# Decay tables of the retention moved from the filter stage to the convolutions; the first normalised input split between VectorE and ScalarE

## The chip, the core and the metric

One core of a Trainium2 chip runs the whole step. The metric is the time of one execution in microseconds on the device, median of several runs. Names of engines: PE is TensorE (matmuls), DVE is VectorE, ACT is ScalarE, POOL is GpSimd, SP issues most DMAs.

## What is computed

Two layers of a hybrid mixer, for a prompt of 128 tokens and a sample of 512, both of width 1024. Cut to what matters here:

```python
def mixer_layer(x, mod, ..., filt, norm_g, w_in, ret_logit, ...):
    h = rmsnorm(x, norm_g) * (1 + scale) + shift
    z = h @ w_in                                  # 5120 columns
    ret_out, ret_s = retention_mixer(q, k, v, ret_logit, ret_s0)
    hy_out = hyena_mixer(zh, hy_conv_w, hy_conv_b, filt, hy_bias)
    lru_out, lru_s = rglru_mixer(...)
    y = concat(ret_out * silu(g_r), hy_out * silu(g_h), lru_out * silu(g_l))
    return x + gate * (y @ w_out), ret_s, lru_s

def retention_dir(q, k, v, log_gamma, state0):    # forward and backward, 4 heads
    dmat = where(diff >= 0, exp(log_gamma * max(diff, 0)), 0)   # 128 x 128 a head
    zeta = exp(log_gamma * (C - 1 - idx))
    xi = exp(log_gamma * (idx + 1.0))
    chunk_decay = exp(log_gamma * C)
    ...
# hyena_filters: a small network over L positions gives two filters a channel;
# the long convolutions with them are done by transforms, twice in a row
```

`dmat`, `xi`, `zeta` and `chunk_decay` are the decay tables. They hang on the weight `ret_logit` alone, so they can be made at any time before the retention.

## The kernel before

All activations lie channels first, with prompt and sample side by side: a tile of 128 channels has 644 columns (128 + 512 and pads). The input projection runs in 40 tiles of output channels (`mtile`; tile names `z0_16` and so on, layer and number, `z_16` for short). Products are kept near full precision by splitting each operand into a high part and a low part: `w_16h`, `w_16l`, and for the normalised input `hh` and `hl`, eight tiles each. A projection tile is 48 matmuls of 322 columns.

Layer 0 goes through these stages. First come a sine network (`hidden`), the norm of the input (`norm0`) and the modulation (`ada_gen`); `make_h0` then makes `hh` and `hl`: for each of eight tiles an affine step from `x` into `t` in two pieces (128 and 512 columns), the high part on ACT, the low part as a difference. Then the filter stage (`filters`): four units `u` one after the other, each with taps (tile `hg`, line 630), a normalisation of them (lines 634 to 645), transposes (`ft`), a fold (lines 508 to 515), splits (`blocks`, line 540) and transforms (`spr`, `spi`). Projection tiles run in between on PE. Then the convolutions (`hy_conv`), in two halves of the channels with two convolutions each, 00 and 01 and then 02 and 03: a fold, splits, five classes that are transformed (`u020` and so on), multiplied by the filter's spectrum (lines 971 to 979), and transformed back (`ie`, `ip`, `io`), and a tail (lines 1047 to 1070) that gives the input of the next fold. Then retention (`ret`) and the recurrent branch (`lru`), head by head, and the output projection.

What sets the order: the work is written as Python generators. `pump` and `until` step those that are due by a planner's clock `clk`, which each matmul advances by its own computed length; a generator says at each `yield` how long it should sleep by that clock. `queue` ties every matmul behind the one before, so PE runs exactly in the order in which the generators issue. `join(t)` steps the generators until `t` is done, and sets the clock forward where nothing is due. The other engines' orders are made by a scheduler from priorities (the order of issue) and dependencies; each engine then takes its instructions strictly in that order.

The tables before: `decays` (some 55 instructions of 8 to 32 columns on DVE) turns the logits into the scales of the exponentials; the scheduler puts it at the program's start. `ret_tables` is a generator started with a delay of 40 (`LTB`) as the layer begins; `ret_table` makes one layer's tables in two steps (directions), each with eight ACTIVATEs of 258 columns on ACT, three tensor_scalar or products on POOL and two steps of 1032 columns on DVE (lines 1111 and 1112), and writes them to DRAM. `prep`, which comes before the convolutions, waits for it and loads them back (`load_tables`).

## Time and profile before

| | us |
|---|---|
| median of 3 runs (1309.91 to 1315.7) | 1310.69 |
| the profiled execution | 1310.14 |
| its span, first to last instruction | 1308.4 |
| PE busy in it | 1159.8 (89%) |
| DVE busy | 896.8 (69%) |
| POOL busy | 627.4 (48%) |
| ACT busy | 590.3 (45%) |

The profiled execution is 0.6 us under the median; 1.7 us of it lie outside the span. Reading: PE is busy for most of the span, but the stages have different limits, so a share of the span says little; what matters is, stage by stage, how long each engine works and what PE waits for.

### The profile page before, as it was taken

Reading aid. Unit: us, or ns where it says so; the run is one execution under the profiler, and the core shown is the slowest. Engines: PE = TensorE matmul, PEld = TensorE weight load, DVE = VectorE, ACT = ScalarE, POOL = GpSimd, SP = SyncE. Lnnn points to the kernel's source line nnn. Section 1 sums busy time; section 2 is a strip of 40 time slices with the busy share of each in tenths; the row PEclk is TensorE's granted clock in tenths of the full one; section 3 lists DMA queues with packets and bytes.
Section 4 is the critical chain, followed back from the end, with each engine's and each line's share of the span. In section 5 each row is a group of like instructions: output and inputs, shape, how many; then the busy total and the mean of one; then the engine's idle time right before and its main releaser. Section 6 shows DMA issues by size and latency. Waiting matters only on the chain. (4 is left out here: it accounts for less than half of the span.)

```text
span 1308.4 us, 20560 instructions
## 1 busy us (share of the span) xinstructions
PE 1159.8 (89%) x7944; PEld 1102.3 (84%) x7944; DVE 896.8 (69%) x1398; ACT 590.3 (45%) x1067; POOL 627.4 (48%) x523
## 2 busy tenths in 40 slices
PE   4588688998998988898989899999999889889996
PEld 2377678998998988897888788999998889879996
DVE  6998976666686776667888775566567587676313
ACT  3567556333333654465565554332333356555221
POOL 2754645544555543634343355544355474445431
PEclk9799879999999988899999989999999899889998
DMA  9642234232211111243545354222221111113222
GB/s 332 218 158 81 80 104 139 93 104 74 73 57 61 41 45 45 79 141 115 176 143 186 122 211 143 79 66 92 77 75 49 53 57 49 47 57 124 64 70 81
DMA packets 53313, 132.79 MB, mean 101 GB/s; under 512 B 6278, under 2 KB 15126, under 8 KB 51936
## 3 DMA queue, kind: packets, MB, share of 16 engines
q1 hardware_dynamic: 52868, 131.38, 30.3%
q8 instruction: 62, 1.02, 0.3%
q14 instruction: 35, 0.29, 0.1%
q10 hardware_dynamic: 348, 0.11, 0.0%
HBM read 112.77 MB, written 18.70 MB: 100 GB/s over the span
## 5 line engine op out<-in xcount | busy, mean ns | idle before, releaser
L298 ACT ACTIVATE r<-arena 128x512 fp32r<-128x512 f32 (+1 forms) x72 | 43.5, 606 | 106.9 <-DVE arena L515 37.6
L298 ACT ACTIVATE arena<-arena 128x644 f32<-128x644 f32 (+6 forms) x88 | 66.1, 766 | 50.4 <-DVE arena L1381 28.6
L298 ACT ACTIVATE rt<-arena 128x512 fp32r<-128x512 f32 (+2 forms) x44 | 29.7, 675 | 77.2 <-POOL arena L976 50.3
L540 POOL TENSOR_TENSOR r<-arena,r 128x512 fp32r<-128x512 f32 (+1 forms) x24 | 29.9, 1245 | 71.6 <-ACT r L298 55.3
L330 PE MATMUL u<-r,cfwd 128*128 128x256 f32 x432 | 61.0, 290 | 2.1 <-DVE r L540 1.9
L330 PEld LDWEIGHTS u<-r,cfwd 128*128 128x128 f32 x432 | 56.8, 197 | 2.8 <-DVE r L540 2.1
L1381 DVE SCALAR_TENSOR_TENSOR arena<-o,arena 128x128 f32<-128x128 f32 (+3 forms) x34 | 16.7, 524 | 56.0 <-PE o L330 56.0
L330 PE MATMUL spr<-r,cfwd 128*128 128x256 f32 x192 | 37.4, 306 | 18.9 <-DVE rt L630 7.6
L971 DVE TENSOR_TENSOR arena<-u,arena 128x512 f32<-128x512 f32 x40 | 27.5, 687 | 38.0 <-PE u L330 36.8
L330 PEld LDWEIGHTS spr<-r,cfwd 128*128 128x128 f32 x192 | 29.4, 199 | 25.5 <-DVE rt L630 9.1
L976 POOL TENSOR_TENSOR arena<-arena 128x256 f32<-128x256 f32 x40 | 36.8, 920 | 21.8 <-DVE arena L972 12.2
L1300 POOL MEMSET arena<- 128x2 f32 x32 | 2.1, 100 | 86.3 <-ACT arena L298 86.3
L979 POOL TENSOR_TENSOR rt<-arena,rt 128x512 fp32r<-128x512 f32 x24 | 31.4, 1308 | 23.9 <-ACT rt L298 23.9
L298 ACT ACTIVATE r<-rt 128x512 fp32r<-128x512 f32 (+3 forms) x50 | 28.2, 564 | 23.2 <-PE spi L330 11.9
L979 DVE TENSOR_TENSOR rt<-arena,rt 128x512 fp32r<-128x512 f32 x16 | 20.4, 1277 | 24.3 <-ACT rt L298 24.3
L298 ACT ACTIVATE arena<-z 64x512 f32<-64x512 f32 (+1 forms) x42 | 26.5, 630 | 23.5 <-PE z L330 23.1
L330 PE MATMUL hg<-r 128*128 128x320 f32 x128 | 26.3, 343 | 11.8 <-DVE r L587 9.5
L540 POOL TENSOR_TENSOR r<-rt,r 128x256 fp32r<-128x256 f32 (+1 forms) x16 | 20.1, 1256 | 34.5 <-ACT r L298 27.8
L330 PE MATMUL spi<-r,cfwd 128*128 128x256 f32 x168 | 34.8, 297 | 1.2 <-DVE rt L630 1.2
L1152 DVE TENSOR_TENSOR rt<-rt,arena 128x512 f32<-128x512 f32 x16 | 23.8, 1490 | 17.4 <-POOL arena L1151 17.4
L1199 DVE TENSOR_TENSOR arena<-rs,dm 128x512 f32<-128x512 f32 (+1 forms) x16 | 7.1, 486 | 40.7 <-PE rs L330 40.7
L298 ACT ACTIVATE arena<-lg,arena 128x322 f32<-128x322 f32 x64 | 30.3, 529 | 10.4 <-PE lg L330 10.1
(1269 smaller groups left out, 4285.8 us busy)
## 6 DMA issues: line engine op xcount, KB each, us to landing
w<-in_w_in SPq DMA_DIRECT2D x80, 512.0 KB, 3.9
aw<-in_ada_w SPq DMA_DIRECT2D x96, 256.0 KB, 5.2
wo<-in_w_out SPq DMA_DIRECT2D x32, 384.0 KB, 3.3
spec<-arena SPq DMA_DIRECT2D x16, 640.0 KB, 3.3
arena<-spec SPq DMA_DIRECT2D x8, 1280.0 KB, 5.4
arena<-in_xT SPq DMA_DIRECT2D x16, 320.0 KB
rt<-in_c_win SPq DMA_DIRECT2D x4, 640.0 KB, 6.3
arena<-xspill SPq DMA_DIRECT2D x8, 320.0 KB, 3.5
```

What stands on the lines that cost most here:

```text
L298: return S.activation(out, in_, f, bias=bias, scale=scale)
L330: return queue(T.matmul(out, lhs, x, start=start, stop=stop), w * n / 2400 * (4 if x.dtype == F32 else 1))
L540: eng.tensor_tensor(lo, src, f(h), op=ALU.subtract)
L971: V.tensor_tensor(y, pv, hre[:, c].unsqueeze(1).broadcast_to([P, 2, 256]), op=ALU.mult)
L976: G.tensor_tensor(y[:, 1], y[:, 1], m2[:, 0], op=ALU.add)
L979: (G if PY >> c & 1 else V).tensor_tensor(lo, yo, f(h), op=ALU.subtract)
L1152: V.tensor_tensor(q, q, ar(sw, 512), op=ALU.add)
L1199: V.tensor_tensor(ar(SC_R + 128 * s0, 128 * nb).rearrange("p (n c) -> p n c", n=nb), ps[:, 0:128 * nb].rearrange("p (n c) -> p n c", n=nb) ...
L1300: G.memset(ar(tt[d] + c, 2), 1.0)
L1381: V.scalar_tensor_tensor(x, zc(ps, pc, pc + n), ar(mod_[l] + 32 + 2 * mt + s, 1), x, op0=ALU.mult, op1=ALU.add)
```

## The change

Four things. (1) `decays` is now the first thing that `ret_tables` issues, and its scratch has moved from the region `HS_` to `ZB_`, where `norm0` keeps its sum (`ACC_`). (2) `ret_tables` starts when `prep` of layer 0 is through, so beside the convolutions. It works in pieces of two heads instead of four (516 columns, twice as many pieces); three steps a piece that POOL did are now two ACTIVATEs on ACT and, for the masks, POOL products of 256 columns; its scratch is in `ZB_`, and it sleeps 6 (`LTE`) of the planner's clock after each of three steps a piece. (3) `prep` of layer 0 no longer waits for the tables; they are joined and loaded behind the `join(c0)` that ends the first half's convolutions. (4) In `make_h0` all eight low parts are on DVE (five were on POOL), the affine steps of tiles 1, 4 and 6 are on ACT (only that of tile 1 was), the high parts of tiles 4 and 5 are made from `t` and no longer from `x` again, and the whole has a raised priority; the split of the transform's constants (`load_cf`) and of the second weight tile are ordered behind it.

```diff
-PG1, PH, LG, NR0, NR1, NR2, NK0, NXV = 6, 182, 4, 1, 0, 2, 2, 68
-NXS, XH, XDE, XG, XW, XL0, XL1, XP = 8, 48, 1, 0, 1, 4, 0, 0
-XQ, PW3, PA0, NA, NV, NQ, PO, PFO = 1, 0, 2, 14, 225, 1, 0, 1
+PG1, PH, LG, NR0, NR1, NR2, NK0, NXV = 6, 0, 4, 1, 0, 2, 2, 68
+NXS, XH, XDE, XG, XW, XL0, XL1, XP = 8, 0, 1, 0, 1, 4, 0, 0
+XQ, PW3, PA0, NA, NV, NQ, PO, PFO = 1, 0, 82, 14, 225, 1, 0, 1
...
-LTB, XSEQ, ... = 40.0, 'FNAAAAAABANBAFBBBBABBB', ...
+LTE, XSEQ, ... = 6.0, 'FNAAAAAABANBAFBBBBABBB', ...
...
-    spx_ = HS_ + 128
+    spx_ = ZB_ + 128
...
-    tA_, tB_, tC_, tD_ = (HS_ + 32 * i for i in range(4))
+    tA_, tB_, tC_, tD_ = (ZB_ + 32 * i for i in range(4))
...
     def ret_tables():
-        gd, mkt = slot("rgrid"), slot("rmask")
-        nc.sync.dma_start(gd[:, 0:516], c_ret[:, 0:516])
-        nc.sync.dma_start(mkt[:, 0:256], c_ret[:, 516:772])
-        yield 3
+        decays()
+        gd, mkt = ar(ROPE_, 516), ar(ROPE_ + 516, 256)
+        nc.sync.dma_start(ar(ROPE_, 772), c_ret)
+        yield 4
         for l in range(DEPTH):
-            yield from ret_table(l, gd, mkt, slot(f"rd{l}")[:, 0:512])
+            for hp in range(2):
+                yield from ret_table(l, hp, gd, mkt)
...
+    def ret_table(l, hp, gd, mkt):
+        d = ar(ZB_ + 1032, 256)
         zg = ar(zgs_[l], 16).rearrange("p (i c) -> p i c", i=8)
+        e0, t0 = ar(ZB_, 516), ar(ZB_ + 516, 516)
         for di in range(2):
+            for h in range(2):
+                col = 16 * l + 8 + 4 * di + 2 * hp + h
                 src = gd[:, 258 * di:258 * di + 258]
+                act(t0[:, 258 * h:258 * h + 258], src, AF.Tanh, scale=ar(sp2_ + col, 1))
+                act(e0[:, 258 * h:258 * h + 258], src, AF.Exp, scale=ar(spm4_ + col, 1))
-            G.tensor_scalar(e0, e0, 0.5, 0.5, op0=ALU.mult, op1=ALU.add)
-            yield 3
+            act(e0, e0, scale=0.5, bias=ar(half_, 1))
+            yield LTE
             V.scalar_tensor_tensor(t0, t0, 1.0, e0, op0=ALU.add, op1=ALU.mult)
             V.scalar_tensor_tensor(e0, t0, 2.0, e0, op0=ALU.subtract, op1=ALU.mult)
-            G.tensor_scalar(t0, e0, -2.0, -1.0, op0=ALU.mult, op1=ALU.add)
-            yield 3
+            act(t0, e0, scale=-2.0, bias=ar(neg1_, 1))
+            yield LTE
...
             if di:
+                G.tensor_tensor(e[:, :, 0:128], e[:, :, 0:128], mk, op=ALU.mult)
+                G.tensor_tensor(d2, d2, e[:, :, 0:128], op=ALU.add)
+            else:
+                G.tensor_tensor(d2, e[:, :, 0:128], mk, op=ALU.mult)
...
+            yield LTE
...
     ada_init()
-    if not XDE:
-        decays()
...
-    last = make_h0()
+    with tc.high_priority(offset=400):
+        last = make_h0()
...
             at = spawn(ada_gen(0, 2))
-            tt0 = spawn(ret_tables(), LTB)
+            tt = []
...
         def prep(l, ft):
             while not (ft.done and at.done):
                 yield 0.5
-            while not tt0.done:
-                yield 0.5
-            load_tables(l)
+            if l:
+                load_tables(l)
             conv_consts()
+            if l == 0:
+                tt.append(spawn(ret_tables(), LTE))
             yield LP
...
         join(c0)
+        if l == 0:
+            join(*tt)
+            load_tables(0)
         nc.sync.dma_start(ar(ROPE_, 1024), c_rope)
```

In the kernel before, `decays` was issued by the line `if XDE: decays()` behind `make_h0`, which the change deletes too.

**PE at the end of the first half's convolutions.** Here `u020` and `u022` are the first transforms of convolution 02, `z0_33` is a projection tile, and `rt1` holds the constants of the transforms back. Before, the projection tiles `z0_32`, `z0_33` and so on come first and the convolution's matmuls lie between theirs:

```order
L330 MATMUL z0_33_3081<-hh00_415,w0_33h_3077 128x322 x2
L330 MATMUL z0_33_3081<-hl00_416,w0_33h_3077 128x322 x2
L330 MATMUL u020_3086<-r1_97,cfwd_96 128x256 x12
L330 MATMUL z0_33_3081<-hh01_418,w0_33h_3077 128x322 x2
L330 MATMUL z0_33_3081<-hl01_419,w0_33h_3077 128x322 x2
L330 MATMUL u022_3112<-r1_97,cfwd_96 128x256 x12
L330 MATMUL z0_33_3081<-hh02_421,w0_33h_3077 128x322 x2
L330 MATMUL z0_33_3081<-hl02_422,w0_33h_3077 128x322 x2
L330 MATMUL z0_33_3081<-hh03_424,w0_33h_3077 128x322 x2
```

Now the same engine behind the last transpose of the second half's input (`ht013p`):

```order
L334 MATMUL ht013p_2979<-arena_72,x103_2542 128x128
L331 MATMUL u020_2993<-r1_97,cfwd_96 128x256 x12
L331 MATMUL u022_3015<-r1_97,cfwd_96 128x256 x12
L331 MATMUL ie02a_3039<-rt1_1972 128x256 x12
L331 MATMUL u021_3052<-r1_97,cfwd_96 128x256 x6
L331 MATMUL ie02b_3072<-rt1_1972 128x256 x12
L331 MATMUL u023_3088<-r1_97,cfwd_96 128x256 x12
L331 MATMUL ip02_3107<-rt1_1972 128x256 x2
```

and where the second half's last convolution ends:

```order
L331 MATMUL io03b_3372<-rt1_1972 128x256 x2
L331 MATMUL io03b_3372<-r1_97,rt1_1972 128x256
L331 MATMUL io03b_3372<-rt1_1972 128x256
L331 MATMUL z0_32_3414<-hh00_417,w0_32h_3410 128x322 x2
L331 MATMUL z0_32_3414<-hl00_418,w0_32h_3410 128x322 x2
L331 MATMUL z0_32_3414<-hh01_420,w0_32h_3410 128x322 x2
```

All matmuls of convolutions 02 and 03 now stand in one piece, and the eight projection tiles `z0_32` to `z0_35`, `z0_38`, `z0_39`, `z0_0` and `z0_4`, between which they lay, follow behind them.

**DVE ahead of `make_h0`.** The rows with their waits: `L630` takes in the taps of the first unit, `L618` splits weights, `L634` and `L635` begin the normalisation; before:

```order
L630 TENSOR_TENSOR rt_98<-hg_314,rt_98 128x320 [waits DVE_49,PE_49]
L630 TENSOR_TENSOR rt_98<-hg_318,rt_98 128x320 [waits DVE_49,PE_49]
L630 TENSOR_TENSOR arena<-hg_324,rt_98 128x320 [waits PE_49]
L630 TENSOR_TENSOR arena<-hg_328,rt_98 128x320 [waits PE_49]
L618 TENSOR_TENSOR r_97<-w_163,r_97 128x256 [waits DMAHW2_49,DMAHW1_49,Activation_49]
L634 TENSOR_SCALAR arena<-arena 128x4 [waits Activation_49]
```

Now (`L633` is line 630 of before, `L399` and `L400` are the copies at the head of `decays`, `L411` to `L414` its next steps; POOL's 18th signal is that of the sixth and last product of `norm0` with the sum in `ACC_`):

```order
L633 TENSOR_TENSOR rt_98<-hg_316,rt_98 128x320 [waits DVE_49,PE_49]
L633 TENSOR_TENSOR rt_98<-hg_320,rt_98 128x320 [waits DVE_49,PE_49]
L399 COPY arena<-arena 128x8 [waits DVE_49,Pool_49]
L633 TENSOR_TENSOR arena<-hg_326,rt_98 128x320 [waits PE_49]
L633 TENSOR_TENSOR arena<-hg_330,rt_98 128x320 [waits PE_49]
L400 COPY arena<-arena 128x8
L399 COPY arena<-arena 128x8
L400 COPY arena<-arena 128x8
L621 TENSOR_TENSOR r_97<-w_165,r_97 128x256 [waits DMAHW2_49,DMAHW1_49,Activation_49]
L411 SCALAR_TENSOR_TENSOR arena<-arena 128x32 [waits DVE_49]
L412 TENSOR_SCALAR arena<-arena 128x32 [waits DVE_49]
```

The first copy of `decays` waits for POOL, in the middle of the taps of the first unit; 27 instructions of `decays` now stand ahead of the first affine step of `make_h0`.

## Rows read from the trace of the kernel before

**Rows 1.** Busy time by stretch: length, PE, PEld, DVE, ACT, POOL, PEclk, DMA share, GB/s.

```profile
34.20:71.10 36.90, 21.27 (x141) 16.99 (x137) 35.69 (x48) 19.16 (x37) 30.54 (x25) 0.77 0.50 177
71.10:105.93 34.83, 31.16 (x236) 26.92 (x237) 30.50 (x58) 26.55 (x64) 14.61 (x11) 1.00 0.55 182
105.93:151.26 45.33, 34.80 (x230) 31.09 (x230) 39.38 (x67) 27.42 (x70) 23.99 (x16) 0.89 0.20 70
151.26:198.72 47.46, 36.31 (x210) 34.02 (x211) 39.85 (x66) 24.03 (x57) 23.21 (x17) 0.82 0.31 104
...
224.70:319.84 95.14, 90.61 (x647) 88.65 (x646) 56.02 (x79) 31.34 (x46) 52.85 (x40) 1.00 0.31 107
319.84:411.60 91.76, 86.91 (x610) 85.49 (x609) 62.98 (x87) 30.36 (x46) 46.72 (x35) 0.98 0.18 58
...
460.00:470.00 10.00, 7.75 (x31) 7.31 (x32) 6.63 (x8) 1.63 (x5) 4.16 (x4) 0.53 0.29 80
```

**Rows 2.** What PE waited for between 105.93 and 198.72: total us, times, longest.

```profile
PE ft L333 <- DVE rt L645: 9.6, 2, 5.4
PE spr L330 <- DVE rt L630: 4.8, 2, 3.4
```

**Rows 3.** The tables' steps: min/median/max ns and starts; what ACT waited for there.

```profile
L1111 DVE SCALAR_TENSOR_TENSOR arena<-arena x4: 1234/2924/3382, 104.5 to 166.6; 128x1032 f32<-128x1032 f32 x4
...
L298 ACT ACTIVATE arena<-rgrid,arena x32: 493/503/522, 95.0 to 166.0; 128x258 f32<-128x258 f32 x32
...
  POOL arena L1113: 6.8, 3
```

**Rows 4.** Timeline, POOL and DVE ahead of `make_h0`: start us, us, engine, line, operation.

```profile
34.23 9.30 POOL L1484 TENSOR_TENSOR arena<-arena 128x640 f32<-128x640 f32 x6 [5.61 <-ACT arena L298]
...
4.25 0.18 DVE L410 TENSOR_SCALAR arena<-arena 128x32 f32<-128x32 f32 x1
...
4.47 0.18 DVE L411 TENSOR_SCALAR arena<-arena 128x32 f32<-128x32 f32 x1
...
25.16 0.68 DVE L642 TENSOR_SCALAR rt<-rt,arena 128x512 f32<-128x512 f32 x2
...
41.06 2.87 DVE L642 TENSOR_SCALAR arena<-arena 128x512 f32<-128x512 f32 x2
...
45.94 3.97 DVE L785 TENSOR_SCALAR t<-arena 128x128 f32<-128x128 f32 x5
```

**Rows 5.** Timeline: a low part of `h` on DVE and one on POOL.

```profile
50.29 0.81 DVE L788 TENSOR_TENSOR hl<-t,hh 128x644 fp32r<-128x644 f32 x1
...
64.04 1.73 POOL L788 TENSOR_TENSOR hl<-t,hh 128x644 fp32r<-128x644 f32 x1
```

**Rows 6.** Timeline of convolution 02: single steps on DVE, ACT, POOL and PE.

```profile
322.92 0.68 DVE L508 TENSOR_TENSOR arena<-arena 128x512 f32<-128x512 f32 x1
...
325.47 0.42 DVE L513 SCALAR_TENSOR_TENSOR arena<-arena 128x256 f32<-128x256 f32 x1
...
341.20 0.69 DVE L971 TENSOR_TENSOR arena<-u,arena 128x512 f32<-128x512 f32 x1 [2.12 <-PE u L330]
...
365.98 1.22 DVE L1065 TENSOR_TENSOR arena<-arena 128x1024 f32<-128x1024 f32 x1
...
336.37 0.63 ACT L298 ACTIVATE rt<-arena 128x512 fp32r<-128x512 f32 x1 [0.19 <-POOL arena L976]
...
340.71 1.31 POOL L979 TENSOR_TENSOR rt<-arena,rt 128x512 fp32r<-128x512 f32 x1 [3.12 <-ACT rt L298]
...
338.86 1.59 PE L330 MATMUL ie02a<-rt 128*128 128x256 f32 x12
```

**Rows 7.** Timeline of PE: starts of projection tiles 32 and 33.

```profile
319.84 0.54 PE L330 MATMUL z<-hh,w_32h 128*128 128x322 f32 x2
...
327.09 0.46 PE L330 MATMUL z<-hh,w_33h 128*128 128x322 f32 x2
```

**Rows 8.** Timeline of PE behind the convolutions: the first value transpose of the retention.

```profile
424.62 1.12 PE L333 MATMUL rv00s<-arena 128*128 128x128 f32 x4 [4.11 <-ACT arena L298]
```

More of the change, by code (lines that the diff above doesn't have):

```diff
@@ L201 @@
 SM_ = XI_ + 1024
-NSM = 624
+NSM = 628
 TOT = SM_ + NSM
@@ L305, in step_kernel @@
     eps_ = small(1)
+    half_, neg1_ = small(1), small(1)
     def raw_tile(nm):
@@ L383, in step_kernel @@
     G.memset(ar(eps_, 1), EPS)
-    spx_ = HS_ + 128
+    G.memset(ar(half_, 1), 0.5)
+    G.memset(ar(neg1_, 1), -1.0)
+    spx_ = ZB_ + 128
     sp_ = small(32)
@@ L788, in make_h0 @@
             b = (G if PH >> k & 1 else V).tensor_tensor(HL[k], t, f(HH[k]), op=ALU.subtract)
-            if PH >> k & 1:
-                lastg = b
-        return a, lastg
+        return a, b
     TB = (CT_, CT_ + HC, ZB_ + 650, ZB_ + 650 + HC)
@@ L1099, in ret_table @@
+    def ret_table(l, hp, gd, mkt):
+        d = ar(ZB_ + 1032, 256)
         zg = ar(zgs_[l], 16).rearrange("p (i c) -> p i c", i=8)
+        e0, t0 = ar(ZB_, 516), ar(ZB_ + 516, 516)
         for di in range(2):
-            eb = Y_
-            rb = eb + 1032
-            for h in range(4):
-                col = 16 * l + 8 + 4 * di + h
+            for h in range(2):
+                col = 16 * l + 8 + 4 * di + 2 * hp + h
                 src = gd[:, 258 * di:258 * di + 258]
-                act(ar(eb + 258 * h, 258), src, AF.Tanh, scale=ar(sp2_ + col, 1))
-                act(ar(rb + 258 * h, 258), src, AF.Exp, scale=ar(spm4_ + col, 1))
@@ L1114, in ret_table @@
-            yield 3
-            e = t0.rearrange("p (h c) -> p h c", h=4)
-            mk = mkt[:, 128 * di:128 * di + 128].unsqueeze(1).broadcast_to([P, 4, 128])
-            t = ar(rb, 512).rearrange("p (h c) -> p h c", h=4)
-            G.tensor_tensor(t if di else d4, e[:, :, 0:128], mk, op=ALU.mult)
-            if di:
-                G.tensor_tensor(d4, d4, t, op=ALU.add)
-            z = zg[:, 4 * di:4 * di + 4]
+            act(t0, e0, scale=-2.0, bias=ar(neg1_, 1))
+            yield LTE
@@ new lines, in ret_table @@
+            e = t0.rearrange("p (h c) -> p h c", h=2)
+            mk = mkt[:, 128 * di:128 * di + 128].unsqueeze(1).broadcast_to([P, 2, 128])
+            d2 = d.rearrange("p (h c) -> p h c", h=2)
+            if di:
+                G.tensor_tensor(e[:, :, 0:128], e[:, :, 0:128], mk, op=ALU.mult)
+                G.tensor_tensor(d2, d2, e[:, :, 0:128], op=ALU.add)
+            else:
+                G.tensor_tensor(d2, e[:, :, 0:128], mk, op=ALU.mult)
+            z = zg[:, 4 * di + 2 * hp:4 * di + 2 * hp + 2]
@@ L1122, in ret_table @@
             V.tensor_scalar(z[:, :, 0], e[:, :, 256], 128.0 ** -0.5, None, op0=ALU.mult)
             V.tensor_copy(z[:, :, 1], e[:, :, 257])
-            nc.sync.dma_start(d_tab[l][:, 512 * di:512 * di + 512].rearrange("p (h c) -> p h c", h=4), e[:, :, 128:256])
-        nc.sync.dma_start(d_tab[l][:, 1024:1536], d)
+            o = 512 * di + 256 * hp
+            nc.sync.dma_start(d_tab[l][:, o:o + 256].rearrange("p (h c) -> p h c", h=2), e[:, :, 128:256])
+            yield LTE
+        nc.sync.dma_start(d_tab[l][:, 1024 + 256 * hp:1280 + 256 * hp], d)
@@ L1494, in step_kernel, with load_cf @@
     a0, a1 = ada_gen(0, 0, True), ada_gen(0, 1, True)
-    def load_cf(last=None):
+    def load_cf(last=()):
         cs = ar(SP_, NCF)
@@ L1499, in load_cf @@
         i = act(CF[:, 0:NCF], cs)
-        if last is not None:
-            behind(i, last)
-        V.tensor_tensor(CF[:, NCF:2 * NCF], cs, f(CF[:, 0:NCF]), op=ALU.subtract)
+        j = V.tensor_tensor(CF[:, NCF:2 * NCF], cs, f(CF[:, 0:NCF]), op=ALU.subtract)
+        for a, b in zip((i, j), last):
+            behind(a, b)
         cf_there.append(1)
@@ L1511, in step_kernel @@
         prefetch(0, MT_HV + 1)
-    last = make_h0()
+    with tc.high_priority(offset=400):
+        last = make_h0()
     if XW:
-        prefetch(0, MT_HV + 1, None, last)
+        prefetch(0, MT_HV + 1, None, last[:1])
     ft = spawn(fg)
     hd = spawn(hidden(1), LHD0)
-    if XDE:
-        decays()
     if not cf_there:
-        load_cf(last[0])
+        load_cf(last)
     for l in range(DEPTH):
```

5 lines of the change are left out of this document (1 added, 4 removed).

## Prediction

> **What bounds the kernel now.** I read the page first, then a table of busy times by stage, then in each stage what PE waited for, and the timelines at the four places the change touches. The page's shares (PE 89%) hide that the stages differ. Ahead of the filters and within their units 1 and 2, PE works for 21.3 of 36.9, 34.8 of 45.3 and 36.3 of 47.5 us at a mean granted clock of 0.77, 0.89 and 0.82, while DVE is busy 84 to 97% [rows 1]: DVE sets the pace, and PE's longest waits there end with DVE's tap normalisation [rows 2]. In both halves of the convolutions PE works for 90.6 of 95.1 and 86.9 of 91.8 us at nearly the full clock, with DVE at some 60 to 70% [rows 1]: PE sets the pace, because projection tiles fill every latency of a convolution. So table work taken out of the filters is worth time, table work put into the first half mostly hides, and fill that is taken away from a convolution costs.
>
> **The change, part by part.** The profiled execution (1310.1, 0.6 under the median) is what the sum is made against.
>
> *Start, +0.5.* Without `decays` DVE finishes the sine network some 3 us sooner, but PE's order and the modulation's weights behind it stay, so I count nothing. Next, the first copy of `decays` now stands in front of two instructions of the first unit's taps and waits for POOL's sixth product, which ended at 34.23 + 9.30 = 43.5 [rows 4]; with DVE quiet POOL may be done at 42.5, and I take 43. Today those instructions run from 37.92 and the first affine step from 45.94 [rows 4], 8.0 later; of these some 2.2 were the normalisation's tensor_scalar pair, 2.87 beside POOL where it takes 0.68 alone [rows 4], and about 1.4 a wait for ACT and weight work, which the new instructions can fill. The 27 instructions of `decays` follow each other every 0.22 [rows 4], some 5.5 us, of which about 1.5 fall into that wait. So the first affine step comes at 43 + 8.0 - 2.2 - 1.4 + 4 = 51.4, 5.5 later than today. From there DVE needs five affine tiles at 0.68, eight low parts at 0.81 [rows 5] instead of five at POOL's 1.73 [rows 5], and 1 us of `decays`: 51.4 + 3.4 + 6.5 + 1 = 62.3, where the last low part now comes at 65.8. But the high part of the first weight tile now stands behind five high parts on ACT, so PE starts the tile late and at the lower clock, and ends it when it does today. The first filter transform then starts at 71 to 72, against 71.1: +0.5, between -5 (the copy waits for nothing that matters) and +4.
>
> *Filter units 1 and 2, -20.* The tables' steps lie between 95.0 and about 170 [rows 3], in these units. Unit 0, which has nearly none, takes 34.8 us; units 1 and 2 take 45.3 and 47.5 [rows 1]. At unit 0's pace they would give back 23.2. Four of the eight long DVE steps took 2.92 us in the median, where 1.23 is their least [rows 3], and ACT stood 6.8 us waiting for POOL's part of the tables [rows 3], with filter work queued behind it. PE's own work in a unit (31.2 in unit 0) does not allow much less than 34. Lower end: 10, the DVE instructions alone without their delays; upper end: 25. I take 20, nearest the comparison of units.
>
> *Tables beside the first half's convolutions, +6.* There come 32 ACTIVATEs at 0.50 [rows 3], 16 rescaling ones of 516 columns at about 0.6, as a 512-column one takes 0.63 [rows 6], and 16 DVE steps of half of 1.23 [rows 3]: 26 us on ACT, which has 64 idle, 10 us on DVE, which has 39 idle [rows 1]. They are hidden by projection tiles as long as nothing that a convolution waits for stands behind them. Not all is: each piece reuses one scratch, so ACT stands until POOL and the table's DMA have read the last one, twice as often as today's 6.8 [rows 3]. All hidden is 0; all of twice 6.8 exposed is 14; I take 6, since PE's fill in this stage has little slack.
>
> *Second half's convolutions without fill, +33.* The join sets the planner's clock forward by 24 sleeps of 6, over 140 us. During that time the planner issues the whole of convolutions 02 and 03, and the eight projection tiles come behind them. PE must now sit through every link. One convolution, from the rows [rows 6]: fold 3.4 (its seven starts lie 0.3 to 0.6 apart, from 322.92 to 325.47), splits 0.63 + 0.69: 4.7. Transform of class 0 1.5 (12 matmuls; 1.59 in the row), two products 1.3, POOL's two steps 1.4, high part 0.63, low part 0.69: 10.2. First inverse 1.5, class 1 0.8, its DVE steps 2.0, POOL 0.7, ACT 0.63, low part on POOL 1.31: 17.2. Prompt 0.7, class 4 1.5, products 1.3, POOL 1.5, ACT and DVE 1.3: 23.5. Last inverse 1.5: 25.0. Tail with ACT, DVE, POOL and the product of 1.22: 29.6. Some 25 hand-overs add 1.2. 7.5 us of it are PE's, and PE would be busy for under half of the stretch: the granted clock was 0.77 where it was busy 58%, and 0.53 in another stretch [rows 1]. I take 0.7, which adds 3.2: 34.0 from fold to fold, 29.4 to the end of the last one. Fold 02 starts 3.1 behind the start of the stretch. Then come eight tiles at 7.25 (from 319.84 to 327.09 [rows 7]): 3.1 + 34.0 + 29.4 + 58.0 = 124.5 where the stretch now takes 91.8 [rows 1]. +33. Lower end +15: not less than DVE's own work, 63 us in the stretch [rows 1] less some 14 for tiles and the convolution before. Upper end +57: the convolutions take as long as now, and all the fill is added.
>
> *Behind the convolutions, -5.* Today PE waits 4.1 us for ACT, which may not overwrite what the last tail still reads [rows 8], and runs at half its clock for a while after. With the convolutions 58 us back, this goes: between -3 and -7.
>
> Sum: 0.5 - 20 + 6 + 33 - 5 = +14.5, so 1324.6; with the 0.6 to the median 1325.
>
> **Rivals.** *The second half at DVE's pace.* If DVE always has the other class's work while one waits, the unfilled stretch costs +12 to +15 rather than +33 and the time is 1304 to 1307; together with a filter gain of 25, under 1303. For it: DVE is the engine with the most work there. Against: a convolution hands over five times through DVE, POOL, ACT and PE in strict order, and its first and last 5 us have nothing beside them. It decides at +25: below that the gain in the filters and behind cancels the loss, and the kernel is not slower; below +12 it is faster.
>
> *Half clock through the whole unfilled stretch.* The granted clock falls to 0.53 in rows of busy but broken work [rows 1]. If it stays at 1.2 GHz throughout, PE's 7.5 us a convolution double: 8.6 more than in the sum for both, +41 there, 1333. By the Trainium skill ("TensorE: Matmul & The Clock Gate", What's actually happening) half rate is the default state and activity lifts it, so a thinly used PE would stay there; the trace agrees in the one stretch at 0.53, but 0.77 at 58% busy is in between. Against: the transforms come in pieces of up to 4 us.
>
> *The tables' steps block the first half.* Twelve POOL steps of some 0.7 (half of the 1.31 [rows 6]) meet DVE; what POOL does to DVE is seen in 2.87 for 0.68 [rows 4]. If each holds up DVE for its length and ACT's waits are all exposed, the first half costs +20 instead of +6: 1339. By the Trainium skill ("SBUF — State Buffer", Who interferes with whom) the port pair shared by these two is an exclusive lock and the loser waits the whole instruction; that row agrees. Against: DVE is idle for 39 of 95 us there [rows 1].
>
> *The first `h` does not come earlier at all*, for the POOL wait: that is in the sum already; were the wait harmless, 5 less.
>
> **Chances.** A change within 0.5%, 6.5 us, can hardly be told from none. Forecast (1318 to 1331) 0.42; half clock 0.14 and blocked tables 0.12, both slower: slower 0.68. DVE's pace: 0.17 within 6.5 us of 1310.7, 0.15 faster, where a larger filter gain or a harmless start goes with it. For 8 in 10 I go down to 1302, where DVE's pace meets the greater filter gain, and up to 1346, where the forecast has two of its terms at the upper end.
>
> **What would show it.** Right: in the profile after, PE waits for DVE, POOL and ACT in convolutions 02 and 03, with PE under 50% busy for some 65 us and a granted clock of about 0.7, then eight tiles without a gap; units 1 and 2 of the filters at 34 to 37 us; a DVE wait for POOL ahead of `make_h0`. Wrong: if the unfilled stretch with its tiles takes less than 110 us, the loss is oversized; if units 1 and 2 stay above 40 us, DVE's table work was not what held them; if the first half grows by over 10 us, the tables are not hidden.

## The result and the profile after

The changed kernel takes 1332.55 us (median of 4 runs, 1330.94 to 1333.29) against 1310.95 of the kernel before: a ratio of 1.0156, 95% interval 1.0129 to 1.0182, so 1.6% slower. The profiled execution took 1333.29, its span is 1331.5, 23.1 more than before.

The stages of the profile after, in the cut that the landmarks of PE give (first transform of each filter unit, first transform of the convolutions, last transpose of the second half's input, last transform back, first key transpose of the retention, first gate product of the recurrent branch). The columns are those of [rows 1].

```profile
34.20:75.23 41.03, 18.67 (x131) 15.10 (x131) 34.76 (x88) 18.87 (x36) 19.10 (x18) 0.75 0.60 220
75.23:112.26 37.03, 32.38 (x236) 28.60 (x237) 30.87 (x59) 22.07 (x54) 12.38 (x9) 0.95 0.39 137
112.26:144.84 32.58, 32.22 (x231) 28.96 (x231) 27.66 (x59) 21.67 (x53) 12.04 (x9) 0.95 0.18 67
144.84:179.29 34.45, 30.48 (x210) 28.06 (x210) 29.96 (x57) 19.83 (x48) 14.36 (x10) 1.00 0.26 90
179.29:223.75 44.46, 40.31 (x266) 38.84 (x267) 28.38 (x44) 33.10 (x53) 27.75 (x17) 0.96 0.32 112
223.75:314.76 91.01, 79.83 (x544) 77.14 (x542) 64.67 (x100) 47.33 (x78) 50.19 (x43) 0.94 0.32 107
314.76:383.51 68.75, 39.69 (x224) 35.36 (x225) 43.13 (x75) 14.97 (x27) 26.36 (x26) 0.78 0.06 20
383.51:448.53 65.02, 65.02 (x440) 65.01 (x440) 21.96 (x27) 20.84 (x26) 28.29 (x20) 1.00 0.22 72
448.53:451.39 2.86, 2.86 (x24) 2.86 (x22) 1.93 (x4) 0.77 (x2) 1.50 (x1) 1.00 0.15 19
```

And the three stretches of the kernel before that [rows 1] cut otherwise, in the same cut:

```profile
198.72:240.07 41.35, 39.30 (x266) 37.58 (x267) 23.11 (x36) 21.02 (x35) 23.20 (x14) 1.00 0.43 153
240.07:320.08 80.01, 75.48 (x546) 73.52 (x545) 52.71 (x75) 26.95 (x42) 42.61 (x34) 1.00 0.24 80
320.08:411.60 91.52, 86.67 (x608) 85.25 (x607) 62.74 (x87) 30.12 (x46) 46.72 (x35) 0.98 0.18 58
```

| stage | before | after | difference | predicted |
|---|---|---|---|---|
| to the first filter transform | 71.10 | 75.23 | +4.1 | +0.5 |
| filter unit 0 | 34.83 | 37.03 | +2.2 | 0 |
| filter units 1 and 2 | 92.79 | 67.03 | -25.8 | -20 |
| unit 3, up to the convolutions | 41.35 | 44.46 | +3.1 | in the next |
| first half of the convolutions | 80.01 | 91.01 | +11.0 | +6 |
| second half, to the first key transpose | 99.72 | 133.77 | +34.1 | +33 |
| from there to the recurrent branch | 9.16 | 2.86 | -6.3 | -5 |
| the rest (880 us) | 879.44 | 880.11 | +0.7 | 0 |
| sum | 1308.4 | 1331.5 | +23.1 | +14.5 |

The first and the last rows of the sum are counted from the span's start and to its end. The last 880 us are the same work in both.

*The second half.* What PE waited for in the 68.75 us of the two unfilled convolutions (total us, times, longest):

```profile
PE u L331 <- ACT r L298: 18.5, 2, 10.5
PE ip L331 <- POOL rt L980: 1.9, 2, 1.0
PE ie02a L331 <- ACT rt L298: 1.3, 1, 1.3
PE ie03a L331 <- ACT rt L298: 1.3, 1, 1.3
```

The gap at the head of each convolution, fold and splits, is the largest: 18.5 us in two waits. PE is busy for 39.69 of 68.75 at a mean granted clock of 0.78; then nine projection tiles (the eight and `z0_8`, which stood behind the convolutions before, too) run for 65.02 us without a gap at 1.00. Before, the tiles lay in the gaps of the convolutions: 86.67 of 91.52 busy (third row of the fence above). So the gaps grew from 4.9 to 29.1 us, 24 of the 34 by which the second half grew; the other 10 are the same matmuls at a lower clock. The clock was at its lower level (0.50) for the first transforms of each convolution, behind the two long waits, and at its upper one from 330.72 to 340.00:

```profile
322.69:328.69 6.00, 5.86 (x24) 5.27 (x24) 2.28 (x4) 0.42 (x1) 1.82 (x3) 0.50 0.00 0
330.72:340.00 9.28, 7.54 (x56) 6.93 (x57) 7.20 (x13) 2.49 (x4) 5.28 (x5) 1.00 0.00 1
357.01:363.01 6.00, 5.86 (x24) 5.27 (x24) 2.28 (x4) 0.42 (x1) 1.82 (x3) 0.50 0.01 3
```

*The start.* DVE of the kernel after, from the copy that waits for POOL to the fold of filter unit 0 (start, length, operation):

```profile
41.67 0.26 DVE L399 COPY arena<-arena 128x8 f32<-128x8 f32 x1 [5.52 <-POOL t L778]
...
50.53 2.22 DVE L788 TENSOR_SCALAR t<-arena 128x128 f32<-128x128 f32 x6
...
60.95 5.04 DVE L791 TENSOR_TENSOR hl<-t,hh 128x644 fp32r<-128x644 f32 x3
...
66.65 2.02 DVE L1502 TENSOR_TENSOR cfwd<-arena,cfwd 128x1792 fp32r<-128x1792 f32 x1
68.58 0.69 DVE L511 TENSOR_TENSOR arena<-rt 128x512 f32<-128x512 f32 x1
...
71.59 2.45 DVE L518 SCALAR_TENSOR_TENSOR arena<-arena 128x256 f32<-128x256 f32 x1
```

The copy stands for 5.52 us, until POOL's sixth product has ended at 41.63 (the row names the MEMSET of `t` that follows it). The first affine step comes at 50.53 instead of 45.94 [rows 4], and the fold (`L511` to `L518`) at 68.58, behind the last low parts. Some of DVE's steps are long: four of 32 columns took 2.92 us at 57.90, three low parts 5.04 at 60.95 (one alone 0.82) and the fold's last 2.45, each while POOL made the low part of a weight tile:

```profile
58.12 2.44 POOL L827 TENSOR_TENSOR w_16l<-w,w_16h 128x1024 fp32r<-128x1024 f32 x1 [16.22 <-ACT w_16h L298]
60.95 3.07 POOL L827 TENSOR_TENSOR w_17l<-w,w_17h 128x1024 fp32r<-128x1024 f32 x1 [0.40 <-ACT w_17h L298]
...
69.14 4.61 POOL L827 TENSOR_TENSOR w_20l<-w,w_20h 128x1024 fp32r<-128x1024 f32 x1 [3.83 <-issue]
```

PE stands for 3.96 us ahead of the first transform, for ACT's copies of the last transposes (`rt<-ft`); on ACT these stand behind the split of that fold, which waited 4.14 us for DVE:

```profile
71.00 0.27 PE L334 MATMUL ftp<-arena 128*128 128x128 f32 x1
75.23 0.99 PE L331 MATMUL spr<-r,cfwd 128*128 128x256 f32 x5 [3.96 <-ACT rt L298]
...
74.07 0.63 ACT L298 ACTIVATE r<-arena 128x512 fp32r<-128x512 f32 x1 [4.14 <-DVE arena L518]
74.60 0.58 ACT L298 ACTIVATE rt<-ft 128x512 f32<-128x512 f32 x1
```

*The first half.* PE's waits ahead of the transforms back of convolution 00 and of projection tile 36 are the new ones, and on ACT the tables' steps stand between the splits. First PE, from 223.75 to 314.50; then four rows of ACT at the head of convolution 00, and ACT's work on the tables' steps from 179.29 to 314.76 by form (count, busy us, mean ns, and what ended its idle time before them):

```profile
PE z L331 <- DVE x L915: 2.2, 1, 2.2
PE ie00a L331 <- ACT rt L298: 2.1, 1, 2.1
...
PE ie00a L331 <- DVE rt L980: 1.6, 1, 1.6
```

```profile
225.13 0.91 ACT L298 ACTIVATE arena<-arena 128x258 f32<-128x258 f32 x2 [3.01 <-DMA tab<-arena]
...
229.95 2.06 ACT L298 ACTIVATE arena<-arena 128x258 f32<-128x258 f32 x4
231.91 0.61 ACT L298 ACTIVATE r<-arena 128x512 fp32r<-128x512 f32 x1
232.43 0.61 ACT L298 ACTIVATE rt<-arena 128x512 fp32r<-128x512 f32 x1
```

```profile
L298 ACT ACTIVATE arena<-arena 128x258 f32<-128x258 f32 x32 | 15.3, 502 | 5.0 <-DMA tab<-arena 3.0 <-DVE arena L1125 1.8
L298 ACT ACTIVATE arena<-arena 128x516 f32<-128x516 f32 x16 | 11.6, 726 | 10.5 <-DVE arena L1112 10.3
L298 ACT ACT_TABLE_LOAD x7 | 9.0, 1283 | 0.1
```

The 32 exponentials and tangents (258 columns) stood 4.8 us for the scratch, until the transfer and a copy (`L1125`) had read the last piece; the rescaling steps (516 columns) behind DVE's second table step (`L1112`) stood 10.3 us for its result, which they work on. Seven loads of ACT's function tables came with the steps; where the tables were made before, in the filters, there was one, and before's stretch from 198.72 to 320.08 has none.

Before, the first half had 75.48 us of PE in 80.01, 4.5 of gaps; after, 79.83 in 91.01, 11.2 of gaps. So 6.7 of the 11.0 are gaps and 4.3 are the same matmuls at a lower granted clock (0.94 instead of 1.00); eleven matmuls of `ie00a`, behind the waits of 2.1 and 1.6, took 2.72 us, 1.56 before.

### The profile page after: what moved, and what is told of

The parts are those of the page before. It is cut to its first block, busy times and chain, and to the rows that moved or that the text cites. A ratio compares the mean times of both kernels' runs of the same rounds, so it can differ in the third digit from the quotient of the medians.

```text
span 1331.5 us, 20601 instructions
## 1 busy us (share of the span) xinstructions
PE 1164.1 (87%) x7944; PEld 1105.1 (83%) x7944; DVE 877.6 (66%) x1415; ACT 609.6 (46%) x1090; POOL 605.1 (45%) x516
## 5 line engine op out<-in xcount | busy, mean ns | idle before, releaser
L298 ACT ACTIVATE arena<-arena 128x258 f32<-128x258 f32 (+6 forms) x136 | 92.9, 699 | 62.1 <-DVE arena L1385 29.3
L331 PE MATMUL u<-r,cfwd 128*128 128x256 f32 x432 | 66.4, 308 | 18.8 <-ACT r L298 18.5
L331 PEld LDWEIGHTS u<-r,cfwd 128*128 128x128 f32 x432 | 61.7, 214 | 19.9 <-ACT r L298 18.9
L980 POOL TENSOR_TENSOR rt<-arena,rt 128x512 fp32r<-128x512 f32 x24 | 31.1, 1296 | 24.0 <-ACT rt L298 24.0
L543 POOL TENSOR_TENSOR r<-rt,r 128x256 fp32r<-128x256 f32 (+1 forms) x16 | 22.6, 1410 | 35.7 <-ACT r L298 29.1
L915 DVE SCALAR_TENSOR_TENSOR lr<-z,arena,lr 128x643 f32<-128x643 f32 (+1 forms) x24 | 21.2, 884 | 20.6 <-ACT lr L298 20.2
```

Of the source, the lines that this page charges most:

```text
L298: return S.activation(out, in_, f, bias=bias, scale=scale)
L331: return queue(T.matmul(out, lhs, x, start=start, stop=stop), w * n / 2400 * (4 if x.dtype == F32 else 1))
L543: eng.tensor_tensor(lo, src, f(h), op=ALU.subtract)
L915: V.scalar_tensor_tensor(u[:, a:b], zc(ps, a + d, b + d), w, u[:, a:b], op0=ALU.mult, op1=ALU.add)
L980: (G if PY >> c & 1 else V).tensor_tensor(lo, yo, f(h), op=ALU.subtract)
```

## Experiments

All times are medians, all ratios are to the kernel before, measured beside each run, with a 95% interval. "To the key transpose" is the second half of the table above.

**1. Shorter sleep.** Theory A: the loss is the unfilled second half. Rival B: the tables' work beside the convolutions is the loss wherever it stands.

```diff
-LTE, ..., LT0 = 6.0, ...
+LTE, ..., LT0 = 2.8, ...
```

> The change with the tables' sleep at 2.8 instead of 6, nothing else: all 24 steps are issued before the join that ends the first half's convolutions, so the join finds the tables done, sets no clock forward, and the eight projection tiles lie between the links of convolutions 02 and 03 again. Theory A (what the change loses, it loses in the unfilled second half): from the last transpose of the second half's input to the first key transpose of the retention it takes 98 to 103 us instead of 133.8; the wait behind the convolutions that the change had removed may come back (0 to 5 us); the time is about 1302 (1296 to 1308), under the kernel before. Rival B (the tables' own work beside the convolutions is the loss, wherever it stands): the first half, 91.0 us in the change and 80.0 before from its first transform to its last transpose, grows beyond 100 because the steps come denser, and the time stays at or above 1325.

1306.35 (0.9955, 0.9940 to 0.9970): 26 us under the change, inside A's range but 4 above its centre, and B falls. The first half stayed at 91.1. To the key transpose it took 106.5, more than A's 98 to 103: the convolutions end 91.8 us after the last transpose, as before (91.5), but with `z0_33` no longer ahead of the first transform of convolution 02 one tile more is left for behind. That tile covers the wait behind the convolutions, which did not come back (2.9), so the two stretches together are 109.4 against 108.9 of the kernel before.

**2. Late join.**

```diff
         join(c0)
-        if l == 0:
-            join(*tt)
-            load_tables(0)
-        nc.sync.dma_start(ar(ROPE_, 1024), c_rope)
...
         rts = []
+        if l == 0:
+            join(*tt)
+            load_tables(0)
+        nc.sync.dma_start(ar(ROPE_, 1024), c_rope)
         for h in range(4):
```

(and the sleep at 4.5)

> The change with the join of the tables, their loading and the loading of the rotation constants moved from behind the first half's convolutions to just ahead of the retention's inputs, and a sleep of 4.5: the tables' steps spread over both halves, and the convolutions of the second half are filled with projection tiles as before. Theory A (the unfilled second half is the loss): first half 84 to 89 us (fewer steps beside it than in the change), second half to the first key transpose 99 to 105, time 1296 to 1308. Rival B (the tables' work beside convolutions is the loss): first half back at 80 to 83, but the second half, which now has steps too, stays over 115 and the time over 1315.

1307.49 (0.9967, 0.9954 to 0.9981): A again. PE's order is that of the kernel before, to the key transpose 99.7, and the wait behind is back (9.2 to the recurrent branch). But the first half stayed at 91.3, where A expected 84 to 89: the table steps had not moved. The last pair of DVE's table steps ran at 290 us in the change, in run 1 and here alike. The sleep sets when a step is issued, and so decides PE's order, which is tied to the order of issue, and hardly that of ACT, DVE and POOL. (That the scheduler pulls a step forward to the first place where its inputs are there is my reading of it.)

**3. Scales at the start.** Theory C: the first filter transform is late because the raised priority puts the fold behind the low parts. Rival D: the copy that waits for POOL, and the 27 instructions, make it late.

```diff
-    spx_ = ZB_ + 128
+    spx_ = HS_ + 128
...
-    tA_, tB_, tC_, tD_ = (ZB_ + 32 * i for i in range(4))
+    tA_, tB_, tC_, tD_ = (HS_ + 32 * i for i in range(4))
...
     ada_init()
+    decays()
...
-        decays()
         gd, mkt = ar(ROPE_, 516), ar(ROPE_ + 516, 256)
```

> The change with the decay scales computed at the program's start, in their old scratch, as in the kernel before; all else as in the change. Theory C (the start is 4.1 us late because the raised priority puts the fold of the first filter unit behind the low parts of h): the first filter transform stays at 73.5 to 75.5 us, the time at 1330 to 1333. Rival D (the copy that waits for POOL in the middle of the taps, and the 27 scale instructions ahead of the affine steps, make it late): the first filter transform comes at 70 to 72 and the time is 1327 to 1329.

1328.28 (1.0119, 1.0084 to 1.0153), and the first filter transform at 69.48, a little under D's 70 to 72: D. It is the landmark that decides; the interval overlaps with that of the change (1.0129 to 1.0182). DVE of this kernel:

```profile
45.99 2.23 DVE L788 TENSOR_SCALAR t<-arena 128x128 f32<-128x128 f32 x6
...
54.13 6.70 DVE L791 TENSOR_TENSOR hl<-t,hh 128x644 fp32r<-128x644 f32 x3 [0.75 <-ACT hh L298]
60.75 2.01 DVE L1502 TENSOR_TENSOR cfwd<-arena,cfwd 128x1792 fp32r<-128x1792 f32 x1
62.68 0.68 DVE L511 TENSOR_TENSOR arena<-rt 128x512 f32<-128x512 f32 x1
...
67.86 0.42 DVE L518 SCALAR_TENSOR_TENSOR arena<-arena 128x256 f32<-128x256 f32 x1
```

The order is that of the change (low parts, constants, then the fold), everything 4.5 to 5.9 us earlier, and PE follows by 5.75. Theory C, which I held, falls.

**4. The new `make_h0` alone.** In the kernel before: `PH` 0, `XH` 0, `PA0` 82, the raised priority and the two orderings behind it, as in the change's diff; nothing else.

> The kernel before with the new division of make_h0 alone: all low parts on VectorE, three affine tiles on ScalarE, raised priority, the constants' split behind it; the tables stay in the filter stage. Theory C (the new make_h0 delays the fold of the first filter unit): the first filter transform comes at 73 to 75 instead of 71.1, units 1 and 2 stay at about 45 and 47 us, the time is 1312 to 1317. Rival D (the new make_h0 by itself is a gain that the scale instructions spoil): the first transform at 66 to 70, the time 1305 to 1310.

1309.17 (0.9982, 0.9965 to 1.0000): the first transform at 69.04 and units 1 and 2 at 45.6 and 45.6 us by the landmarks of the table (45.3 and 47.5 before). D again. The new division brings the first transform forward by 2.1; the time is no more than 0.35% lower.

**5. Both repairs.** The edits of runs 1 and 3 together.

> The change with both repairs at once: the tables' sleep at 2.8 (convolutions 02 and 03 are filled again) and the decay scales at the program's start. If the two costs are separate (fill and start), the gains add: first filter transform at 69 to 70 us, first half about 91, second half to the first key transpose 106 to 107, time 1302 (1299 to 1304). Rival: the units behind give the start back, the time stays at 1305 to 1307.

1302.06 (0.9932, 0.9917 to 0.9946), with the first transform at 70.15, a first half of 91.8 and 106.7 to the key transpose: the two costs add. In medians 26.2 and 4.3 make 30.5, and 30.5 came; by the ratios it is 2.0% and 0.4%, and 2.2% came.

**6. The tables' price.** In run 5, `ret_table` cut to

```diff
     def ret_table(l, hp, gd, mkt):
...
+        if hp == 0:
+            V.tensor_copy(zg, gd[:, 0:16])
+            nc.sync.dma_start(d_tab[l][:, 0:768], ar(ROPE_, 768))
+            nc.sync.dma_start(d_tab[l][:, 768:1536], ar(ROPE_, 768))
+        for k in range(6):
+            yield LTE
```

> The kernel of the run before (sleep 2.8, scales at the start) with all 16 exponentials and tangents a layer, their products and masks left out: three small instructions a layer put other numbers in the tables' place, so the retention is computed with wrong decays; all matmuls stay in their order. It is the price of the tables' steps where they stand now. Theory E (the 11 us by which the first half grew, 80.0 to 91.0, are the steps'): first half 80 to 82, unit 3 to the last transform 24 to 26 instead of 28, time 1286 to 1291. Rival F (half of it comes from something else that moved, such as the prefetches or the freed wait for POOL): first half 85 to 88, time 1294 to 1298.

1283.78 (0.9797, 0.9781 to 0.9814): E. Two rows, first half and unit 3 to its last transform (from the unit's first `spa` matmul to its last `spi`; 24.5 in the kernel before, 27.7 in the change):

```profile
213.63:294.98 81.35, 76.91 (x546) 75.00 (x545) 53.29 (x76) 27.11 (x42) 42.57 (x34) 0.98 0.24 79
172.81:198.09 25.28, 24.10 (x157) 22.61 (x155) 18.68 (x32) 15.54 (x26) 12.74 (x9) 0.93 0.45 166
```

The first half is back at 81.35 with the granted clock at 0.98, unit 3 at 25.3 instead of 28.4. So 13.6 us there are the steps'. In the profiles the rest behind the convolutions is 2.9 shorter too, the start 1.2 and the other units 1.0, which I can't assign; the whole price by the medians is 18.3.

**7. Two scratch regions.** Theory G: ACT standing for the scratch is what holds up convolution 00. Rival H: the steps' own time and place.

```diff
-SM_ = XI_ + 1024
+SM_ = XI_ + 1032
...
-        e0, t0 = ar(ZB_, 516), ar(ZB_ + 516, 516)
         for di in range(2):
+            b = (ZB_, XI_)[di]
+            e0, t0 = ar(b, 516), ar(b + 516, 516)
```

> The kernel with both repairs, and two scratch regions for the tables' steps in turn instead of one, so that ScalarE need not wait until POOL and the transfer to DRAM have read the last piece. Theory G (ScalarE standing for the scratch is what holds up the splits of convolution 00): first half 83 to 88 instead of 91, time 1294 to 1299. Rival H (the steps' own time, and their place ahead of the links of convolution 00, hold it up): first half 89 to 93, time 1300 to 1304.

1298.85 (0.9909, 0.9895 to 0.9924); first half 89.8. The time lies in G's range, the stretch in H's. ACT's waits for DVE's second table step fell from 10.3 us to 3.5, a wait of 3.3 for the transfer stayed, and the first half gave back 2.0 of the 10 that run 6 says are the steps': PE's longest wait for ACT ahead of `ie00a` grew from 2.5 to 5.1 us, with ten of the sixteen long DVE steps, instead of six, now ordered ahead of the first transform's products. The waits taken away explain a small part. Those for DVE were waits for data, not for the scratch; with a second region ACT has the next piece's exponentials to do meanwhile.

**8. Spread.** Run 5 with the late join and the sleep (4.5) of run 2, and

```diff
-                act(t0[:, 258 * h:258 * h + 258], src, AF.Tanh, ...)
+                i = act(t0[:, 258 * h:258 * h + 258], src, AF.Tanh, ...)
+                if h == 0:
+                    tc.add_manual_dep(i.ins, order[1], NOSYNC, reason="order")
```

> The kernel with both repairs, the fill restored by the late join, and each piece's first exponential ordered behind the matmul that was issued last, so that the scheduler can no longer pull the pieces ahead: two pairs of VectorE steps stand before the first transform of the convolutions instead of six, eight beside the second half. Theory H (what costs is where the steps stand: packed around the first links of convolution 00): first half 83 to 87, second half to the first key transpose 99 to 103, time 1292 to 1299. Rival I (every step costs the same wherever it stands beside convolutions): first half and second half together stay at about 191, time 1301 to 1305.

1297.14 (0.9893, 0.9875 to 0.9910). First half 87.0, to the key transpose 103.0, from there 8.3: together 198.3 against 201.4 in run 5. H's direction, at the weak end: some 3 us of the stretches, 4.9 of the medians, and the late join is in these, too. Rival I's stretches came as well (87.0 and 103.0 are 190.0, against its 191); only its time did not. So that the place matters is shown, how much is not. (The expectation's "two pairs" and "six" are single long DVE steps, sixteen in all.)

**9. Spread, later, two scratches.** Runs 7 and 8 together, the generator spawned with 24.0 instead of `LTE`, sleep 4.0.

> The spread kernel (late join, pieces ordered behind the matmul issued last) with two scratch regions in turn, a start that is 24 of the planner's clock after prep instead of one sleep, and a sleep of 4.0: no table step stands before the first two transforms of convolution 00. Theory H (what costs is where the steps stand): unit 3 to the last transform 25 to 26.5 instead of 27.7, first half 82 to 85, second half to the first key transpose 102 to 106, time 1288 to 1294. Rival I (every step costs the same beside convolutions): what the first half gains the second loses, time 1295 to 1299.

1293.63 (0.9864, 0.9846 to 0.9881), in H's range; but unit 3 stayed at 27.7 and the first half at 86.5, both missed. Only the first exponential of a piece was held back: the others, with function table loads of 1.28 us, still ran in unit 3.

**10. Unfilled, with no table moved.** The kernel before with

```diff
         join(c0)
+        if l == 0:
+            join(c1)
         nc.sync.dma_start(ar(ROPE_, 1024), c_rope)
```

> The kernel before with one line more: behind the join that ends the first half's convolutions it also joins the second half's, so that convolutions 02 and 03 are issued in one piece and the eight projection tiles behind them, in the order of the change; the tables stay in the filter stage. Theory A (the missing fill alone makes the change's second half slow): the second half to the first key transpose takes 131 to 136 us instead of 99.7, the wait behind it (6.3) goes as in the change, and the time is 1310.7 + 34.1 - 6.3 = 1338.5 (1334 to 1342). Rival J (a part of the change's 133.8 is its tables' loading and traffic): 118 to 128 us there, time 1322 to 1332.

1338.86 (1.0200, 1.0176 to 1.0224): A, 0.4 above its sum (and 27.1 above the kernel before beside it, 1311.78, where the sum had 27.8); J falls. The two parts of the second half, cut 0.2 us earlier than in the change:

```profile
319.60:388.60 69.00, 39.95 (x227) 35.36 (x225) 43.36 (x75) 15.20 (x27) 26.48 (x26) 0.78 0.05 20
388.60:454.14 65.54, 65.54 (x441) 65.54 (x440) 21.94 (x27) 20.86 (x26) 28.30 (x20) 1.00 0.21 71
```

Row by row this is the change's second half: 69.00 and 65.54 us, PE busy 39.95 at 0.78, then 65.54 at 1.00. The tables have no part in it.

**11. The old `make_h0`.** Run 5 with the division of the kernel before.

> The kernel with both repairs (sleep 2.8, scales at the start) and the division of make_h0 of the kernel before (five low parts on POOL, one affine tile on ScalarE, no raised priority). If the new make_h0 is worth 2 us wherever it stands, as it was alone: first filter transform at 71 to 72.5, time 1304 (1303 to 1306). Rival: with the tables out of the filter units it is worth nothing (the units give it back): 1300.5 to 1302.5; or more than 4, because POOL is then a bound in the units: over 1306.

1298.62 (0.9904, 0.9885 to 0.9922): under both expectations. Its interval overlaps that of run 5 (0.9917 to 0.9946). By the landmarks the first transform comes 2.1 later (72.21 against 70.15), the recurrent branch only 0.8, and the 880 us behind, which are the same work in both, were 1.9 shorter in this profile. So with the tables out of the filters the new division is worth nothing that these runs can show; whether it costs something stays open.

**12. All exponentials held back.** Run 9 with the ordering for all four ACTIVATEs of a piece.

```diff
-                if h == 0:
-                    tc.add_manual_dep(i.ins, order[1], NOSYNC, reason="order")
-                act(e0[:, 258 * h:258 * h + 258], src, AF.Exp, ...)
+                j = act(e0[:, 258 * h:258 * h + 258], src, AF.Exp, ...)
+                for a in (i, j):
+                    tc.add_manual_dep(a.ins, order[1], NOSYNC, reason="order")
```

> The kernel of the run before that spread and delayed the pieces (1293.6), with all four exponentials and tangents of a piece ordered behind the matmul issued last, and not the first alone: in that run three of the four, and their loads of ScalarE's function tables, still stood in filter unit 3 and ahead of the first transform. Theory K (those early exponentials are what unit 3 still pays): unit 3 to the last transform 25 to 26 instead of 27.7, first half 84 to 87, time 1290 to 1292.5. Rival L (unit 3 is longer for another reason, or the first half takes back what unit 3 gains): unit 3 at 27 to 28, or first half over 88; time 1293 to 1296.

1292.74 (0.9833, 0.9806 to 0.9859). Unit 3 fell to 25.3, as K said, and the first half rose to 88.6, as L said; the second half to the key transpose is 99.6 as before. The time, 0.2 above K's range and 0.3 under L's, can't be told from run 9's. It is the fastest kernel of the study that computes the whole reference: 1.7% under the kernel before as measured beside it (1314.8), 1.4% under its 1310.95 beside the change.

## Why the prediction was right, and where it was not

*Direction and range* held: slower, 1332.55 in 1302 to 1346. The forecast's own band (1318 to 1331) was missed by 1.5. Of the 8.6 us by which the sum fell short (23.1 against 14.5), tables +8.1, start and unit 0 +5.8, the filter gain -5.8, the others +0.5. So the sum was helped by one error against another, and of the named signs of being wrong one came: the first half grew by over 10 us.

*Second half's convolutions without fill, +33.* Measured +34.1, and run 10 shows it alone. The chain worked out from single rows gave 34.0 from fold to fold; the first transforms of 02 and 03 lie 322.69 and 357.01, 34.3 apart. The size was right, its parts only in part. The chain counted 7.5 us of PE a convolution and forecast PE under 50% busy; it was busy for 39.69 of 68.75, 58%, since all of a convolution's 112 matmuls run there and not the chain's alone. The granted clock was taken as 0.7 and was 0.78, so that 10 of the 34 us are slower matmuls where the chains had 6.4 (twice 3.2). The reason for the long join was not right either: the prediction said that the clock goes forward by 24 sleeps, over 140 us. By the planner's own count eleven of the 24 fall inside the first half; the join is reached at 205.6 on its clock and left at 284.3, and in those 79 it waits, but for one last step, for the tables of layer 1, which nothing needs before layer 1. 79 is enough for both convolutions, so the order came out as predicted.

*Filter units 1 and 2, -20.* Measured -25.8, just over the upper end (25). The pace of unit 0 was taken as the limit. Without table steps PE sets the pace in unit 1, 32.22 of 32.58 busy, which [rows 1] did not show in any unit. Run 11, with the old `make_h0` and the tables out, has nearly the same two units (31.1 and 34.5); run 4, with the new `make_h0` and the tables in, keeps 45.6 and 45.6. So the gain is the tables'.

*Start, +0.5.* Measured +4.1 and 2.2 more in unit 0. The first affine step came as worked out (51.4 predicted, 50.53 measured), and projection tile 16 did end where it ended before (its low products end at 68.8, before 68.6). Two steps failed. The last low part was to come at 62.3 and ended at 65.99: the sum took DVE's steps at their length alone, and beside POOL's work on the weights' low parts seven of them took 8.0 us. And the last step, from there to "the first filter transform at 71 to 72", hung the first transform on PE's tile, while it hangs on DVE's fold, which in the new order comes behind all low parts and the constants. DVE is one chain from the norm to that fold, so the 4.6 us of the late first affine step arrive whole: run 3 takes them away and gains 5.75 there. The 2.2 of unit 0 are another matter: the unit stays long in run 3 (37.9), and why is open. Run 3 removes the wait for POOL and the 27 instructions together; the rows tell them apart. The taps behind the copy start at 41.75, in run 3 at 37.97, 3.8 for the wait; from them to the first affine step it is 8.78 against 8.02, only 0.8 for the instructions, since the normalisation's pair no longer meets POOL (0.68 us instead of 2.80).

*Tables beside the first half, +6.* Measured +11.0, and 3.1 in unit 3: 14.1, at the upper end. The mechanism named, ACT standing for the one scratch, is there, but with 4.8 us, where the sum allowed up to 13.6; the longer waits, 10.3, are for DVE's result, and run 7, with two scratches, gained 2 in the stretch and 3.2 in the median. The work was priced too low: 26 us on ACT and 10 on DVE, where the steps took 26.9 on ACT and the sixteen long ones 16.1 on DVE; and the sum left out the seven loads of function tables, 9.0 (run 6, without the steps, has none there). And it did not see the place: the scheduler put six of the sixteen long DVE steps ahead of the products of the first transform, and ACT's exponentials between the splits that the next link needs. How much the place is worth, the runs show in part. All steps cost 18.3 in run 5 by the medians; spread, held back and with two scratches (run 12) 9.3 of these came back, and unit 3 is at 25.3 as in run 6. From the first transform of the convolutions to the recurrent branch run 5 takes 201.4, runs 7, 8, 9 and 12 take 198.7, 198.3, 198.0 and 197.4, and run 6, without the steps, 190.5: 7 to 8 us stay wherever the steps stood, and what they are is open. The table of [rows 1] gave 64 us of idle ACT, but idle time is of no use to a step that stands in front of a split. And a gap costs twice: 6.7 us more of gaps came with 4.3 of slower matmuls.

*Behind, -5.* Measured -6.3; the first value transpose no longer waits [rows 8], and runs 2, 8, 9 and 12, with all fill before the convolutions' end, have the wait back.

*The rivals.* "The second half at DVE's pace" fell: +34, not +12 to +15; DVE was busy for 43.13 of 68.75. "Half clock through the whole stretch" forecast 1333, which is the time that came, but by other terms: the clock was 0.50 at the head of each convolution and 0.78 in the mean. By the Trainium skill ("TensorE: Matmul & The Clock Gate", What's actually happening) half rate is the default that activity lifts; the rows agree, since the clock was at half behind the long waits and at 1.00 in the busier stretch from 330.72 to 340.00. "The tables' steps block the first half" forecast +20 there; +14 is two thirds of the way. The collision that it feared, with POOL's steps of the tables, is not what the longest row shows: DVE's second step at 215.29 took 2.78 us instead of 0.69 while POOL worked on the low part of a weight tile:

```profile
214.64 2.87 POOL L827 TENSOR_TENSOR w_18l<-w,w_18h 128x1024 fp32r<-128x1024 f32 x1
```

```profile
215.29 2.78 DVE L1112 SCALAR_TENSOR_TENSOR arena<-arena 128x516 f32<-128x516 f32 x1
...
226.87 0.69 DVE L1112 SCALAR_TENSOR_TENSOR arena<-arena 128x516 f32<-128x516 f32 x1
```

By the Trainium skill ("SBUF — State Buffer", Who interferes with whom) the loser of the shared port pair waits for the whole instruction of the other; this row agrees, POOL's ends at 217.5 and DVE's 0.6 later.

## What to carry to other kernels

A join in a kernel whose fill is ordered by a planner's clock is not free even where all that it waits for is off the critical path: here it waited for layer 1's tables and cost 34 us of fill (28 net of the wait behind the convolutions, which went), and one number (run 1) brings back 26 us. A join on layer 0's tables alone would by the planner's count be left at 210.5 and not 284.3; no run tried it. Ask of every moved piece of work who has to wait for its scratch: a copy of eight columns that waited for POOL delayed the chain of the start by some 4 us. And when work is moved "beside" a stage that is bound by another engine, look at where the scheduler puts it, and at the function tables that it makes ACT load, not at the idle time of the stage; holding it back with an order-only dependency moved it, a sleep did not.

## What was not expected of the hardware

The mean granted clock of a stretch reacts to few and short gaps: in the first half it was 0.94 with 11.2 us of gaps in 91.01, and 1.00 with 4.5 in 80.01. And a load of ScalarE's function table cost 1.28 us and nothing beyond it: in run 9 one began at 186.17 and the ACTIVATE behind it at 187.47.
